# Deferred operand stores, a row scale on another engine and an earlier query load in a two-layer Fourier and attention encoder

## The chip, the cores and the metric

The kernel runs on one core of a Trainium2 chip. The metric is the device time of one execution in microseconds (us), lower is better. A core has five engines that run side by side, each through its own instructions in the order in which they were put on its queue: TensorE (PE in the profile; its weight loads are PEld), VectorE (DVE), ScalarE (ACT), GpSimd (POOL) and SyncE (SP). SP computes nothing here: it issues nearly all the transfers. An engine whose next instruction waits for a semaphore holds up all that stand behind it on its queue.

## The reference

Two sequences go through the same two layers: the prompt with 1024 tokens and the sample with 512, each token 1024 wide. All is float32.

```python
def swiglu_ffn(x, g, w_gate, w_up, w_down):
    h = rms_norm(x, g)
    return (jax.nn.silu(h @ w_gate) * (h @ w_up)) @ w_down
...
for i in range(DEPTH):                      # DEPTH = 2
    if i % 2 == 0:
        x = x + fourier_mixer(x, ...)
    else:
        x = x + attention_mixer(x, ...)
    x = x + swiglu_ffn(x, norm_ffn[i], ffn_w_gate[i], ffn_w_up[i], ffn_w_down[i])
```

The mixer of layer 0 is a grouped Fourier transform followed by a projection. That of layer 1 is attention with 8 query heads on 2 key and value heads of 128 numbers, with normed and rotated queries and keys. The inner width of the SwiGLU block is 2816, in 22 chunks of 128. Since the norm's factor is one number for each token, it can be applied after a product as well as before it: the kernel multiplies gate and up by the row factor r.

## The kernel before

**Numbers in two parts.** A product is made with three matmuls of reduced-precision float32 (`mm3`, L248 to L251): each operand is split into a high part, a copy cast by ACT (L242), and a low part, the difference, on DVE or, where `eng=pool` is given, on POOL (L243). For the weights of the feed-forward block of the sample, `weights_by` (L278) issues the load on SP (L283), casts on ACT (L287) and subtracts on POOL (L288). The raw weights have two buffers, the split ones four.

**Blocks.** Tokens are worked on in blocks of 512: block 0 is the sample, blocks 1 and 2 the prompt. The sample goes through `ffn` (L759), chunk by chunk. The prompt's two blocks go through `ffn_pair` (L924), which makes products of 2 by 2 blocks with seven multiplications (Strassen's scheme in Winograd's form). Its moving operands, seven sums and differences of the normed residual (`OPERANDS`, L35), are made beforehand by `moving` (L871) and stored to DRAM.

**Stages.** `weave` (L1397) interleaves two generators by estimated costs: a main one, marked "F", and an auxiliary one, marked "X". Layer 0's `ffn(0, 0)` runs beside the prompt's mixer and then beside `moving`. When both have ended, `ffn_pair` of layer 0 has TensorE alone. Its tail overlaps the sample's attention (`qkv`, `attend`). Then the sample's output projection and its feed-forward block of layer 1 run beside the prompt's `qkv`, `attend`, output projection and second `moving`. The second `ffn_pair` ends the kernel.

**Order.** The framework that compiles the program puts instructions on each engine's queue in an order of its own, by estimated readiness, with the written order as priority. Where that order has to hold, the code pins an instruction (`pinned`, L256; `keep` in `ffn_pair`). So what is written earlier is not always queued earlier.

**The places that the change touches:**

- `ffn`, L847 to L856, once per chunk, 22 chunks in each of two layers. When the gate product `ga` is complete in PSUM, DVE multiplies it by r (L851) and ACT takes silu into `s` (L853). When the up product is complete, DVE multiplies it by r (L852) and then by `s` (L854). ACT casts the high part and DVE subtracts the low part of `mid` (L856), which the down products read in the next chunks. r lies in SBUF as `first["r"]`, the tile `ss` in the profile.
- `moving`, L877 to L921, four rounds j. A round loads four pieces of the residual (L883), multiplies them by gain and r on DVE (L889) and makes seven operands with `put` (L892): split, then at once a store to DRAM on SP (L905). Low parts of B21, T1, T3 and N4 are made by POOL. B11 and B21 also stay in SBUF (`ring`). The round hands over to the other generator three times (`yield 5.0`): after B11, B21, B22, after T1, T3, and after T2, N4.
- `ffn_pair`, L1175 to L1218. Each step takes the stationary operand made one step before and prepares the next. Hooks run inside steps: `load_rows_down` (L997) loads two rows of down weights in the step T1. `prepare_down` (L1031) starts `operands_down` (L1003) in the step B22: a split on POOL and the sum `s1` on DVE (L1017). The next part of it (L1019, a difference on POOL, and another split) runs in the step T3. The rest is asked for by `product` (L1041).
- `attend`, L1330 to L1394. At the start of each head the query is loaded (L1333, one or two transfers) and split with a low part on POOL (L1335). Then come, for each chunk of 128 queries, the scores (L1343), the softmax on DVE and ACT (L1348 to L1354), the transposes of the probabilities on PE (L1366) and the products with the values.

Of the kernel before, what the change touches and what calls it, by code (L numbers as in the profile page):

```python
# [24 lines left out]
GROUP = NH // NKV  # L25
# [100 lines left out]
def trunk_kernel(ctx: ExitStack, tc: tile.TileContext, t: dict):  # L126
# [632 lines left out]
    def ffn(layer, b, h, out=None):  # L759
# [50 lines left out]
        for fc in range(NF):  # L810
            f0, odd_ = fc - fc % 2, fc % 2
            wg, wu = ready.pop(("gate", fc)), ready.pop(("up", fc))
            if not odd_ and wds is not None:
                want("B", f0 - 2)
                wds.append(ready.pop(("B", f0 - 2)))
            ga, up = bankg(), bankg()
            for dc in range(NC):
                if odd_ and dc == 4:
                    want("A", f0)
                part(wg, h, ga, dc)  # L820
                if here and fc == 0:
                    part(wu, h, up, dc)
                if not odd_ and dc >= 5:
                    one()
                if dc % 2:
                    yield 1.36 if odd_ or dc < 5 else 2.0 if dc == 5 else 2.7
            if odd_:
                want("gate", fc + 1)
                wds = open_items(ms, f0)
            for dc in range(NC):  # L830
                if not odd_ and dc == 3:
                    want("gate", fc + 1)
                if fc == NF - 1 and dc == 4:
                    want("B", f0)
                if dc == (2 if odd_ else 4):
                    want("up", fc + 1)
                if fc == 0 and not here and dc == 1:
                    settled(b)
                if not (here and fc == 0):
                    part(wu, h, up, dc)  # L840
                if not odd_:
                    one(2 if dc in (2, 4, 6) else 1)
                elif dc >= 6:
                    one()
                if dc % 2:
                    yield (3.4 if dc > 1 else 2.7) if not odd_ else 2.7 if dc == 7 else 1.36
            s = tmp()  # L847
            if fc == 0 and not here:
                first["r"] = tl("ss", [TB], F32, "ssF")
                act.copy(first["r"], in_rows(rstd[b]))  # L850
            dve.tensor_tensor(ga, ga, first["r"], op=ALU.mult)  # L851
            dve.tensor_tensor(up, up, first["r"], op=ALU.mult)  # L852
            act.activation(s, ga, AF.Silu)  # L853
            dve.tensor_tensor(up, up, s, op=ALU.mult)  # L854
            m = tl("mid", [2, TB], F32R, "mid")
            split(m[:, 0], m[:, 1], up)  # L856
            if odd_:
                ms.append(m)
            else:
                ms = [m]  # L860
# [10 lines left out]
    def moving(blocks, gain, out, ring, helped):  # L871

        staging = open_pool("mv")
        yield 2.0
        r = [in_rows(rstd[b]) for b in blocks]
        yield 1.0
        for j in range(4):  # L877
            x4 = tl("x", [2, 2, TB], F32, "wX")
            v = {}
            for k in range(2):  # L880
# [11 lines left out]
            def put(name, src):  # L892
# [9 lines left out]
                        room.extend([two[:, 0], two[:, 1]])  # L902
                    x = room.pop(0)
                split(x[:, 0], x[:, 1], src, eng=pool if name in helped else None)
                sp.dma_start(out[name][:, j], x.bitcast(F32))  # L905

            put("B11", v[0, 0])
            put("B21", v[1, 0])
            put("B22", v[1, 1])
            yield 5.0  # L910
            t1 = x4[:, 0, 0]
            dve.tensor_tensor(t1, v[0, 1], v[0, 0], op=ALU.subtract)
            put("T1", t1)
            dve.tensor_tensor(v[0, 1], v[1, 1], v[0, 1], op=ALU.subtract)
            put("T3", v[0, 1])
            yield 5.0
            dve.tensor_tensor(v[1, 1], v[1, 1], t1, op=ALU.subtract)
            put("T2", v[1, 1])
            dve.tensor_tensor(v[1, 0], v[1, 0], v[1, 1], op=ALU.subtract)
            put("N4", v[1, 0])  # L920
            yield 5.0  # L921
        close_pool("mv")

    def ffn_pair(layer, blocks, ring, places, outs):  # L924
# [250 lines left out]
        for f0 in range(0, NF, 2):  # L1175
# [20 lines left out]
                plus(U[i], ps, U[i])  # L1196
            for i, ps in (yield from step("T1", lambda: load_rows_down(f0), 0)):
                plus(V[i], ps, U[i])
            for i, ps in (yield from step("B22", lambda: prepare_down(f0), 0)):
                plus(ps, ps, V[i])  # L1200
                if i == 0:
                    s = gated(1, W, ps)
                else:
                    finish(1, ps, s)
            for i, ps in (yield from step("T3", lambda: next(preps[-1]), 0)):
                plus(U[i], ps, U[i])
                plus(ps, ps, V[i])
                if i == 0:
                    s = gated(2, V[0], ps)
                else:  # L1210
                    finish(2, ps, s)
            for i, ps in (yield from step("N4", None if f0 else lambda: load_acc(blocks[0], 0), 0)):
                plus(ps, ps, U[i])
                if i == 0:
                    s = gated(3, U[0], ps)
                else:
                    finish(3, ps, s)
# [89 lines left out]
    def attend(blocks, straight, slot):  # L1307
# [6 lines left out]
        for g in range(NKV):  # L1314
# [12 lines left out]
                sp.dma_start(vr[:, n * 4 : n * 4 + 4], dv[b][g][:, :, :])  # L1327
            split(vt[:, 0], vt[:, 1], vr, eng=pool)
            yield 1.0
            for h in range(g * GROUP, (g + 1) * GROUP):  # L1330
                qr = raw_tile(T)
                for n, b in enumerate(blocks):
                    sp.dma_start(qr[:, n * TB : (n + 1) * TB], dqk[b][h][:, :])  # L1333
                qt = w_tile(2, T)
                split(qt[:, 0], qt[:, 1], qr, eng=pool)  # L1335
                pts = {}

                def scores(qc):
# [45 lines left out]
                for qc in range(nk + LAG):  # L1384
                    if qc < nk:
                        ps.append(scores(qc))
                        yield 0.7 * nb
                    n = qc - LAG
                    if n >= 0:
# [294 lines left out]
```

## Time and profile before

| | us |
|---|---|
| median of 3 runs | 2942.33 (2935.05 to 2945.19) |
| profiled execution, its own time | 2943.94 |
| its span, first to last instruction | 2942.2 |
| mean granted clock of TensorE | 0.989 |

The profiled execution took 1.74 us more than its span and 1.61 us more than the median. All the rows quoted below belong to it. "PE" rows are matmuls, one row of `mm3` each on L249, L250 and L251. A tile's name before the arrow is what is written, names behind it what is read: `g<-h,w` is a gate or up product of `ffn`, `c<-mid,w` a down product, `a<-ring,w` a product of `ffn_pair`, `a<-w,w` the scores of the prompt's attention.

### The profile page before, as it was taken

How to read it: one execution, taken by the hardware profiler on the slowest of the kernel's cores; microseconds unless marked ns; L12 is line 12 of the kernel's file. 1: busy time of each engine (PE TensorE's matmuls, PEld its weight loads, DVE VectorE, ACT ScalarE, POOL GpSimd, SP SyncE). 2: the span in 40 equal slices, each digit the busy share in tenths (PEclk: the TensorE clock that was granted, in tenths of full speed). 3: DMA queues.
4: the chain of work that ended last, by engine and by line, in shares of the span. 5: the costliest groups of instructions: out<-in, count | busy, mean ns of one | idle time of the engine just before them, and what ended most of it. 6: DMA issues, size and time to landing. Idle time of an engine off the chain costs nothing.

```text
span 2942.2 us, 37189 instructions
## 1 busy us (share of the span) xinstructions
PE 2851.2 (97%) x13656; PEld 2350.9 (80%) x13656; DVE 1737.2 (59%) x3067; ACT 1307.7 (44%) x2134; POOL 1516.2 (52%) x932
## 2 busy tenths in 40 slices
PE   7999999999999999999999999999998999999999
PEld 6778877788888887787777888888886788888887
DVE  6674554466666666836546565563245466666666
ACT  5543233333333333546757777763233333333332
POOL 4334355676776676432332122224535667766774
PEclk8999999999999999999999999999999999999999
DMA  6435475766556653632322112115447865556553
GB/s 219 147 121 161 133 270 188 274 219 218 199 185 207 229 187 111 232 97 86 94 97 90 35 61 78 54 54 179 161 159 279 303 236 202 186 206 226 197 172 116
DMA packets 178870, 490.53 MB, mean 167 GB/s; under 512 B 19488, under 2 KB 29728, under 8 KB 177280
## 3 DMA queue, kind: packets, MB, share of 16 engines
q1 hardware_dynamic: 177760, 483.36, 48.5%
q0 software_dynamic: 640, 3.74, 0.4%
q8 instruction: 108, 1.77, 0.3%
q10 hardware_dynamic: 288, 1.05, 0.1%
q14 instruction: 74, 0.61, 0.1%
HBM read 422.01 MB, written 66.06 MB: 166 GB/s over the span
## 4 chain that ended last, share of the span: by engine, by line
PE 42%; issue 3%; DVE 3%; POOL 2%; ACT 2%; DMA 2%; SPq 0%; POOLq 0%; DVEq 0%; ACTq 0%
PE a L249 6%; PE a L251 6%; PE a L250 6%; PE c L249 5%; PE c L250 4%; PE c L251 4%; PE g L251 3%; PE g L249 3%; PE g L250 3%; PE c L1366 2%; POOL w L288 1%; DVE col L1349 1%; DMA x<-xres 1%; DVE col L1348 1%; DVE acc L1056 1%
## 5 line engine op out<-in xcount | busy, mean ns | idle before, releaser
L288 POOL TENSOR_TENSOR w<-raw,w 128x1024 fp32r<-128x1024 f32 x200 | 479.2, 2403 | 852.0 <-ACT w L287 828.9
L243 POOL TENSOR_TENSOR w<-raw,w 128x512 fp32r<-128x512 f32 (+1 forms) x464 | 607.1, 1328 | 437.8 <-ACT w L242 430.3
L242 ACT CAST w<-raw 128x512 fp32r<-128x512 f32 (+1 forms) x464 | 279.5, 632 | 533.3 <-PE a L251 174.8
L287 ACT CAST w<-raw 128x1024 fp32r<-128x1024 f32 x200 | 208.3, 1048 | 280.6 <-PE g L251 97.0
L249 PE MATMUL g<-h,w 128*128 128x512 f32 x704 | 281.1, 399 | 11.6 <-ACT w L287 6.9
L251 PE MATMUL g<-h,w 128*128 128x512 f32 x704 | 278.3, 395 | 1.2 <-POOL w L288 1.2
L249 PE MATMUL a<-ring,w 128*128 128x512 f32 x708 | 277.5, 392 | 0.0
L250 PE MATMUL g<-h,w 128*128 128x512 f32 x704 | 277.5, 394 | 0.0
L251 PE MATMUL a<-ring,w 128*128 128x512 f32 x708 | 276.0, 390 | 0.0
L250 PE MATMUL a<-ring,w 128*128 128x512 f32 x708 | 275.8, 390 | 0.0
L1056 DVE TENSOR_TENSOR acc<-g,acc 128x512 f32<-128x512 f32 x294 | 201.7, 686 | 105.2 <-PE g L251 104.9
L1056 DVE TENSOR_TENSOR acc<-c,acc 128x512 f32<-128x512 f32 x294 | 201.6, 686 | 93.2 <-PE c L251 91.5
L249 PE MATMUL c<-mid,w 128*128 128x512 f32 x604 | 237.4, 394 | 13.5 <-ACT mid L242 9.5
L250 PE MATMUL c<-mid,w 128*128 128x512 f32 x604 | 236.7, 392 | 1.3 <-DVE mid L243 1.1
L251 PE MATMUL c<-mid,w 128*128 128x512 f32 x604 | 236.4, 392 | 0.0
L249 PE MATMUL c<-h,w 128*128 128x512 f32 x480 | 191.5, 400 | 4.4 <-ACT h L245 3.5
L250 PE MATMUL c<-h,w 128*128 128x512 f32 x480 | 189.7, 396 | 0.4
L251 PE MATMUL c<-h,w 128*128 128x512 f32 x480 | 189.3, 395 | 0.0
L780 DVE TENSOR_TENSOR acc<-c,acc 128x512 f32<-128x512 f32 x176 | 120.8, 688 | 112.6 <-PE c L251 111.9
L249 PEld LDWEIGHTS g<-h,w 128*128 128x128 f32 x704 | 133.7, 190 | 39.3 <-ACT w L287 7.3
L249 PEld LDWEIGHTS a<-ring,w 128*128 128x128 f32 x708 | 133.1, 188 | 32.2 <-DVE mid L243 4.3
L251 PEld LDWEIGHTS g<-h,w 128*128 128x128 f32 x704 | 133.3, 189 | 29.1 <-POOL w L288 2.0
(393 smaller groups left out, 6712.5 us busy)
## 6 DMA issues: line engine op xcount, KB each, us to landing
ring<-mov_B SPq DMA_DIRECT2D x248, 512.0 KB, 5.5
ring<-mov_T SPq DMA_DIRECT2D x88, 512.0 KB, 5.3
raw<-in_gate_dram SPq DMA_DIRECT2D x44, 512.0 KB, 3.5
raw<-in_up_dram SPq DMA_DIRECT2D x44, 512.0 KB, 3.5
raw<-in_down_dram SPq DMA_DIRECT2D x88, 256.0 KB, 3.0
raw<-in_gate_dram SPq DMA_DIRECT2D x88, 256.0 KB, 5.3
raw<-in_up_dram SPq DMA_DIRECT2D x88, 256.0 KB, 5.6
raw<-in_down_dram SPq DMA_DIRECT2D x44, 512.0 KB, 4.2
```

Of the source, the lines that this page charges most:

```text
L242: keep(act.copy(hi, src))
L243: keep(eng.tensor_tensor(lo, src, hi.bitcast(F32), op=ALU.subtract))
L249: pe.matmul(out, lh, rh, start=first, stop=False, **kw)
L250: pe.matmul(out, lh, rl, start=False, stop=False, **kw)
L251: pe.matmul(out, ll, rh, start=False, stop=last, **kw)
L287: pinned(act.copy(flat[:, 0], raw)) if early else act.copy(flat[:, 0], raw)
L288: pool.tensor_tensor(flat[:, 1], raw, flat[:, 0].bitcast(F32), op=ALU.subtract)
L780: dve.tensor_tensor(acc[dc], box[0], acc[dc], op=ALU.add)
L1056: dve.tensor_tensor(acc, chain[d], acc, op=ALU.add)
L1348: dve.tensor_reduce(st[:, 2 * kb : 2 * kb + 1], sc[:, kb], op=ALU.max, axis=AX.X)
L1349: dve.scalar_tensor_tensor(st[:, 1:2], st[:, 2 * nb - 2 : 2 * nb - 1], st[:, 0:1], nrqc[:, gq, h : h + 1], op0=ALU.max, op1=ALU.mult)
L1366: pe.transpose(tr[:, i * P : (i + 1) * P], p[:, kc * P : (kc + 1) * P], ident)
```

## The change

Four edits are made. In `moving` a store is no longer issued by `put`: it goes to a list, and the list is issued at the start of the next third of the round, after the other generator had its turn. In `ffn` the up product is no longer multiplied by r. Instead, GpSimd multiplies silu's result `s` by r in SBUF, and DVE multiplies the up product by that. In `ffn_pair` the first iteration (f0 = 0) runs both parts of `operands_down` one step later, in T3 and N4 in place of B22 and T3. In `attend` the query of the next head of the same group is loaded and split after half the score chunks of the present head (`nk // 2`), where it was done at the start of its own head.

```diff
@@ ffn
             dve.tensor_tensor(ga, ga, first["r"], op=ALU.mult)
-            dve.tensor_tensor(up, up, first["r"], op=ALU.mult)
             act.activation(s, ga, AF.Silu)
+            pool.tensor_tensor(s, s, first["r"], op=ALU.mult)
             dve.tensor_tensor(up, up, s, op=ALU.mult)
@@ moving
+        stores = []
+
+        def flush():
+            for dst, x in stores:
+                sp.dma_start(dst, x.bitcast(F32))
+            stores.clear()
+
         yield 1.0
         for j in range(4):
+            flush()
...
                 split(x[:, 0], x[:, 1], src, eng=pool if name in helped else None)
-                sp.dma_start(out[name][:, j], x.bitcast(F32))
+                stores.append((out[name][:, j], x))
...
             put("B22", v[1, 1])
             yield 5.0
+            flush()
...
             put("T3", v[0, 1])
             yield 5.0
+            flush()
...
             put("N4", v[1, 0])
             yield 5.0
+        flush()
         close_pool("mv")
@@ ffn_pair
-            for i, ps in (yield from step("B22", lambda: prepare_down(f0), 0)):
+            for i, ps in (yield from step("B22", (lambda: prepare_down(f0)) if f0 else None, 0)):
...
-            for i, ps in (yield from step("T3", lambda: next(preps[-1]), 0)):
+            for i, ps in (yield from step("T3", (lambda: next(preps[-1])) if f0 else lambda: prepare_down(0), 0)):
...
-            for i, ps in (yield from step("N4", None if f0 else lambda: load_acc(blocks[0], 0), 0)):
+            for i, ps in (yield from step("N4", None if f0 else lambda: (load_acc(blocks[0], 0), next(preps[-1])), 0)):
@@ attend
-            for h in range(g * GROUP, (g + 1) * GROUP):
+            def query(h):
                 qr = raw_tile(T)
...
                 qt = w_tile(2, T)
                 split(qt[:, 0], qt[:, 1], qr, eng=pool)
+                return qt
+
+            hq = {g * GROUP: query(g * GROUP)}
+            for h in range(g * GROUP, (g + 1) * GROUP):
+                qt = hq.pop(h)
...
                     if qc < nk:
                         ps.append(scores(qc))
+                        if qc == nk // 2 and h + 1 < (g + 1) * GROUP:
+                            hq[h + 1] = query(h + 1)
```

## The prediction, made before the changed kernel had run

> **What bounds the kernel now.** I read the page first, for the shares of the engines.
>
> ```profile
> span 2942.2 us, 37189 instructions
> PE 2851.2 (97%) x13656; PEld 2350.9 (80%) x13656; DVE 1737.2 (59%) x3067; ACT 1307.7 (44%) x2134; POOL 1516.2 (52%) x932
> L251 PE MATMUL g<-h,w 128*128 128x512 f32 x704 | 278.3, 395 | 1.2 <-POOL w L288 1.2
> ```
>
> TensorE is busy for 2851.2 of 2942.2 us, so it is idle for 91.0 us in all. No edit of the diff takes a matmul away: what the change can win is idle time of TensorE and time at a lower granted clock. The third line shows how little the ordinary feed-forward chunks offer: 704 matmuls of gate and up waited 1.2 us in the whole run for a weight split on POOL. Next I read the table by stretches, to see where the 91 us lie.
>
> ```profile
> core 0: us, PE busy (x) PEld busy (x) DVE busy (x) ACT busy (x) POOL busy (x), PEclk, DMA share, GB/s
> 375.00:450.00 75.00, 68.68 (x292) 55.38 (x291) 42.96 (x67) 29.41 (x44) 45.63 (x26) 0.98 0.76 269
> 550.00:1150.00 600.00, 600.00 (x2640) 493.15 (x2639) 387.22 (x600) 217.79 (x392) 426.06 (x301) 1.00 0.62 210
> 1600.00:2000.00 400.00, 387.02 (x2235) 328.53 (x2235) 242.24 (x450) 284.72 (x405) 98.13 (x41) 1.00 0.18 58
> 2240.00:2260.00 20.00, 11.88 (x37) 8.75 (x36) 10.63 (x16) 6.38 (x10) 9.69 (x6) 0.74 0.79 286
> 2285.00:2300.00 15.00, 10.81 (x38) 8.38 (x36) 4.76 (x7) 1.73 (x3) 10.10 (x6) 0.77 0.73 250
> 2300.00:2915.00 615.00, 615.00 (x2702) 505.30 (x2701) 394.74 (x598) 220.96 (x397) 437.32 (x308) 1.00 0.59 205
> ```
>
> In each row the stretch and its length come first, then busy time by engine. The two pair stages (550 to 1150, 2300 to 2915) have TensorE busy all the time at full clock: nothing can be won there. The reach of the change is the first operand stage (375 to 450, 6.3 us idle), the prompt's attention (13.0), and two short places near the second operand stage (8.1 and 4.2). These two also lose clock: 20 us at 0.74 and 15 us at 0.77 are 5.2 and 3.5 us of work not done. The timeline of PE gives the single gaps in brackets, with who ended them; the third of them is at the start of the first pair.
>
> ```profile
> 415.50 0.47 PE L249 MATMUL c<-mid,w 128*128 128x512 f32 x1 [3.17 <-ACT ring L242]
> 444.98 0.50 PE L249 MATMUL c<-mid,w 128*128 128x512 f32 x1 [2.44 <-ACT mid L242]
> 543.30 0.73 PE L249 MATMUL c<-mid,w 128*128 128x512 f32 x2 [2.15 <-ACT mid L242]
> 2248.16 0.80 PE L249 MATMUL g<-h,w 128*128 128x512 f32 x1 [6.89 <-ACT w L287]
> 2292.23 1.22 PE L249 MATMUL c<-mid,w 128*128 128x512 f32 x2 [4.19 <-ACT mid L242]
> ```
>
> So there are five gaps, 18.8 us together. I take the edits to them one by one.
>
> **Stores a third of a round later.** The gap of 6.89 us waits for the cast of gate weights. The queues of SP and POOL ahead of it:
>
> ```profile
> 2230.51 4.40 SPq L905 DMA_DIRECT2D mov_T<-l  x3
> 2237.86 0.32 SPq L905 DMA_DIRECT2D mov_N<-l  x1
> 2238.22 2.23 SPq L883 DMA_DIRECT2D x<-xres  x4
> 2240.49 0.43 SPq L283 DMA_DIRECT2D raw<-in_gate_dram  x1
> ...
> 2230.43 2.41 POOL L288 TENSOR_TENSOR w<-raw,w 128x1024 fp32r<-128x1024 f32 x1
> 2232.80 1.28 POOL L243 TENSOR_TENSOR l<-x,l 128x512 fp32r<-128x512 f32 x1
> 2234.05 2.53 POOL L243 TENSOR_TENSOR w<-raw,w 128x512 fp32r<-128x512 f32 x2
> 2236.53 1.30 POOL L243 TENSOR_TENSOR l<-x,l 128x512 fp32r<-128x512 f32 x1
> ```
>
> SP stood before the store of N4 until POOL had made its low part (2236.53 + 1.30 = 2237.83), then issued the store, the next round's four loads, and only then the gate weights, at 2240.49. The last weight split on POOL before that ended at 2230.43 + 2.41 = 2232.84, so both raw buffers were free 7.65 us before the load went out. A load that much earlier would close the gap of 6.89 and give back the clock. But does the edit do that? It moves the store of N4 by one turn of the other generator, to a place that is still ahead of the next round's loads, and the gate load stood behind these loads too. The order on a queue is also not the written one:
>
> ```profile
> 1535.20 0.86 SPq L1333 DMA_DIRECT2D raw<-dqk  x2
> ...
> 1545.84 3.15 SPq L1333 DMA_DIRECT2D raw<-dqk  x4
> ```
>
> These rows are the first and the last of the prompt's first four queries: two transfers for the first head, four for the third and fourth, all issued within 14 us though written a head apart. A transfer goes out when the compiler takes it to be ready, and the readiness of a store (its low part on POOL) is not changed by a later place in the program. I therefore cost this edit at nothing, and keep both ends: a loss of 1.3 us (one low part later) and a gain of 6.89 + 5.2 = 12.1 us. Nothing reads what is stored before the pair begins, so a late store itself costs nothing as long as feed-forward chunks are left to cover it.
>
> **Row scale on GpSimd.** 44 multiplications leave DVE, 44 come to POOL. The prices, from the list by lines:
>
> ```profile
> L852 DVE TENSOR_TENSOR g<-g,ss 128x512 f32<-128x512 f32 x44 | 30.6, 696 | 30.7 <-PE g L251 30.3
> L243 POOL TENSOR_TENSOR mid<-f,mid 128x512 fp32r<-128x512 f32 x44 | 56.1, 1297 | 5.4 <-ACT mid L242 5.4
> ```
>
> L852 is 0.70 us. POOL's multiplication of this size isn't in the trace, but its subtraction of two SBUF tiles of 128x512 is, at 1.30 us: I take 1.30, so POOL gets 44 x 1.30 = 57 us more and DVE 30.6 less. It stands beside the up product, so it is off the path as long as POOL comes to it before that product's 24 matmuls have ended; a POOL that comes later delays `mid` by what is missing. From the end of the up product to `mid` one DVE instruction less remains. Where TensorE waits for `mid` the saving is real. At the start of the second pair DVE did this:
>
> ```profile
> 2289.45 0.69 DVE L1017 TENSOR_TENSOR s<-raw,raw 128x512 f32<-128x512 f32 x1 [9.51 <-DMA raw<-in_gate_dram]
> 2290.06 0.69 DVE L852 TENSOR_TENSOR g<-g,ss 128x512 f32<-128x512 f32 x1
> 2290.85 0.70 DVE L854 TENSOR_TENSOR g<-g,t 128x512 f32<-128x512 f32 x1
> ```
>
> L854 would start 0.79 us earlier. The gap of 2.15 us at the start of the first pair has the same line behind it, so I take the same there: 1.6 us won. At the gap of 2.44 us L852 also stands ahead of `mid`, but ACT had other casts in front: between nothing and 0.7, I take 0.4. In the attention stage DVE serves the softmax and L852 sits between:
>
> ```profile
> 375.00:450.00 75.00, 2.77 (x4) 0.98 0.76 269
> 1600.00:2000.00 400.00, 6.96 (x10) 1.00 0.18 58
> 2175.00:2260.00 85.00, 2.77 (x4) 0.94 0.73 265
> 1786.40 0.70 DVE g L852
> PE g L251 <- POOL w L243: 2.1, 4, 0.6
> PE a L251 <- POOL w L243: 1.3, 1, 1.3
> ```
>
> The first three lines count L852 alone: 10 of them between 1600 and 2000, and 4 in each operand stage. The fourth is the one that I found on the chain of waits. Between 0.7 and 7.0 us; since one was on the chain, I take 1.0. Against this stands POOL in the operand stages, where by the rows above it had no pause between 2230.43 and 2237.83. One multiplication there makes the low part of N4, its store and all behind it 1.30 late: between nothing and one for each of the 8 chunks of the two operand stages, 10.4 us. I take one, 1.3, since POOL is busy for 45.63 of 75 us there and has room elsewhere.
>
> **First down operands a step later.** In the rows above L1017, the sum of two down rows, held DVE for 9.51 us until its rows had landed, and `mid` was behind it. If it moved behind L854, both gaps (4.19 and 2.15) and 3.5 us of clock would go: 9.8 us. But it was put there, ahead of a product not yet done, because it was taken to be ready; the rows are loaded where they were, so it should be put there again. I take nothing, with 9.8 less the 1.6 above as the other end.
>
> **Queries half a head earlier.** No transfer is added, only its place changes, and the rows above show them issued far ahead already. The waits for a POOL split of this kind are 2.1 and 1.3 us; I take 1.0 of the 3.4, with nothing and 3.4 as ends.
>
> Sum: -1.6 - 0.4 - 1.0 + 1.3 - 1.0 = -2.7 us. The profiled execution's own time was 2943.94 (span 2942.2 and 1.74 around it): 2941.2. Its median lies 1.61 lower, so 2939.6; I say **2939**.
>
> **The clock.** A gap costs more than its length if the granted clock falls:
>
> ```profile
> 405.00:425.00 20.00, 16.83 (x67) 13.37 (x67) 11.43 (x18) 6.90 (x10) 10.77 (x7) 0.91 0.83 302
> 440.00:452.00 12.00, 9.56 (x43) 7.60 (x42) 10.54 (x17) 6.31 (x11) 9.70 (x6) 1.00 0.85 293
> ```
>
> Around the gap of 3.17 us the clock was 0.91 over 20 us (1.8 us lost), around that of 2.44 it was 1.00. So here the step lies between 2.4 and 3.2 us. The gap of 4.19 becomes 3.40 by the sum above and stays past it: its 3.5 us of lost clock are not won. A gap of 2.44 that grows by one multiplication, to 3.74, would cross it. The Trainium skill (TensorE: Matmul & The Clock Gate, section What's actually happening) has the clock fall after a whole idle window of about 3.4 us. By that rule a gap of 3.40 could leave the clock up, and the sum would be 3.5 us lower; but the gap of 3.17 would then have cost no clock, and the trace shows that it did.
>
> **Rivals.**
> *SP is freed* (faster): the gate load goes out before the late store. For it: both raw buffers stood free for 7.65 us. Against it: readiness sets the order. 12.1 us more: 2939 - 12 = 2927.
> *The down sum moves* (faster): 2939 - 8.2 = 2931. For it: later in the program means lower priority. Against it: it was ready by the estimate.
> *POOL becomes the bound in the operand stages* (slower). The multiplication waits on POOL's queue for silu, and the weight splits and low parts stand behind it. For it: POOL's 7.4 us without a pause ahead of the largest gap. Against: 45.63 of 75. It decides once POOL has no pause in most of the 8 chunks; then 8 x 1.30 = 10.4 us, 1.3 of it already in the sum, and two more falls of the clock at 1.8 to 5.2 us each, say 5: 2939 + 9.1 + 5 = 2953.
> *The clock stays up* after the shortened gap of 3.40 us: 2939 - 3.5 = 2936. Against it: the gap of 3.17.
> *The change does not do what it says*: queues come out as before and POOL's price eats DVE's gain: 2943.
>
> **How the numbers follow.** A measurement of this kernel can tell about 0.3%, 8.8 us, from no change: below 2933.5 is faster, above 2951.1 slower. Chances: forecast 0.40, clock up 0.04, SP freed 0.20, down sum 0.13, POOL 0.17, nothing done 0.06. Faster is SP freed, most of the down sum (0.11) and a tail of the forecast (0.03): 0.34. Slower is most of POOL: 0.14 and a tail of 0.02: 0.16. The rest, 0.50, is the same. The range goes from 2925, below SP freed, to 2954, just above POOL. It leaves out both faster rivals together (2919), and POOL with more than two falls of the clock, under 2 in 10 together.
>
> **What would show it.** Right: 44 rows of POOL at L854's place of about 1.3 us and none of L852; the gap near 2248 still there and ended by the gate cast; L1017 still just ahead of the last up multiplication, with gaps near 3.4 and 1.4 us. Wrong: the gate load ahead of the store of N4 and a clock of 1.00 there (SP freed); L1017 behind `mid`; or weight splits late behind POOL's multiplication, with PE waiting for L288 by more than 1.2 us. The compiler's order may also shift elsewhere, in the 1150 to 1600 stretch above all, for which I have no term.

## The result and the profile after

| | before | changed |
|---|---|---|
| median, us (14 runs each) | 2939.89 (2933.71 to 2945.32) | 2934.45 (2932.45 to 2939.76) |
| ratio, 95% interval | | 0.9983 (0.9975 to 0.9991) |
| profiled execution, us | 2943.94 | 2934.45 |
| its span, mean granted clock | 2942.2, 0.989 | 2932.7, 0.992 |

The change is worth 5 us, 0.17%: inside the 0.3% that counts as no change, yet with an interval below 1. The two profiled executions lie 9.5 us apart because that of before is 4.05 us above the median of its 14 runs and that of the changed kernel is its median. So about 4 us of the difference between the two traces are chance, and the traces have to be compared by stretches.

The page of the changed kernel, whole span: shares of the engines, then groups by line.

```profile
PE 2843.5 (97%) x13656; PEld 2347.7 (80%) x13656; DVE 1717.8 (59%) x3023; ACT 1304.9 (44%) x2134; POOL 1574.1 (54%) x976
...
L249 PE MATMUL c<-mid,w 128*128 128x512 f32 x604 | 238.2, 395 | 16.1 <-ACT mid L242 8.1
L250 PE MATMUL c<-mid,w 128*128 128x512 f32 x604 | 237.3, 393 | 2.9 <-DVE mid L243 2.9
```

TensorE has the same 13656 matmuls. DVE has 44 instructions fewer, POOL 44 more. TensorE stood idle for 16.1 us ahead of the first rows of down products (L249), 8.1 of it waiting for the high part of `mid`, and for 2.9 us ahead of L250, waiting for its low part alone. On the page of before these were 13.5, 9.5 and 1.1 us. The list by lines gives the moved multiplication's price:

```profile
L853 POOL TENSOR_TENSOR t<-t,ss 128x512 f32<-128x512 f32 x44 | 56.8, 1292 | 26.5 <-ACT t L852 26.4
```

Next the table by stretches, first before, then changed. The columns are those of the prediction: the stretch, its length, PE, PEld, DVE, ACT, POOL, granted clock, DMA share and rate. The three stretches are the first operand stage with the start of the first pair, the prompt's attention, and the second operand stage with the start of the second pair.

```profile
375.00:560.00 185.00, 176.53 (x766) 144.11 (x765) 83.15 (x126) 60.94 (x88) 106.40 (x56) 0.99 0.64 221
...
1600.00:2000.00 400.00, 387.02 (x2235) 328.53 (x2235) 242.24 (x450) 284.72 (x405) 98.13 (x41) 1.00 0.18 58
...
2175.00:2320.00 145.00, 131.74 (x555) 105.84 (x555) 72.15 (x119) 50.34 (x80) 84.58 (x50) 0.94 0.76 268
```

```profile
375.00:560.00 185.00, 177.97 (x774) 145.44 (x773) 77.68 (x118) 61.32 (x90) 118.92 (x67) 0.99 0.66 224
...
1600.00:2000.00 400.00, 385.72 (x2217) 326.73 (x2216) 234.17 (x428) 279.12 (x396) 114.60 (x53) 1.00 0.19 61
...
2175.00:2320.00 145.00, 134.50 (x575) 108.45 (x574) 66.95 (x101) 51.09 (x83) 97.45 (x60) 0.96 0.82 288
```

Idle time of TensorE is the length less PE's busy time; clock lost is the length times what is missing to 1.00 (the clock is given in hundredths, so this is good to about 1 us). In the second operand stage idle time falls from 13.3 to 10.5 us and lost clock from 8.7 to 5.8: 5.7 us won. In the first, idle time falls from 8.5 to 7.0: 1.4 won. In attention it rises from 13.0 to 14.3: 1.3 lost.

Something is lost outside the table too. From 95 to 375 us, where the sample's first feed-forward block runs beside the prompt's mixer, idle time rises from 5.0 to 7.4 us. The list of waits of that stretch has a row in the changed kernel that before has not (us in all, times, longest):

```profile
PE c L249 <- DVE acc L780: 2.4, 3, 1.3
```

Three times a down product waits for DVE's running sum of down products. At the longest of these waits, DVE's queue has a mixer instruction (L482) ahead of the sum, where before it had it behind. All eight kernels of this document with GpSimd's multiplication have this row at 2.4 to 2.6 us, the five with the multiplication of before have none. It is a price of the row scale.

The timeline of PE in the changed kernel shows the single gaps, in brackets:

```profile
414.13 0.77 PE L249 MATMUL c<-mid,w 128*128 128x512 f32 x1 [3.75 <-ACT ring L242]
...
441.62 0.50 PE L249 MATMUL c<-mid,w 128*128 128x512 f32 x1 [0.69 <-ACT mid L242]
...
540.31 0.50 PE L249 MATMUL c<-mid,w 128*128 128x512 f32 x1 [1.92 <-ACT mid L242]
...
2241.90 1.22 PE L249 MATMUL c<-mid,w 128*128 128x512 f32 x2 [5.45 <-ACT mid L242]
...
2284.34 0.80 PE L250 MATMUL c<-mid,w 128*128 128x512 f32 x1 [2.69 <-DVE mid L243]
```

Against before: 3.17 became 3.75, 2.44 became 0.69, 2.15 became 1.92, 6.89 became 5.45 and is now a wait for `mid` in place of gate weights, and 4.19 became 2.69, a wait for the low part only.

The fourth stretch lies between the end of the first pair and attention. The same two matmuls stand at its ends in both kernels, first before, then changed:

```profile
1210.93 0.50 PE L249 MATMUL a<-mid,w 128*128 128x512 f32 x1 [1.73 <-DVE acc L1056]
...
1516.78 1.22 PE L317 MATMUL c<-dg,ones 128*128 128x128 f32 x4 [2.20 <-ACT t L1277]
```

```profile
1208.34 0.50 PE L249 MATMUL a<-mid,w 128*128 128x512 f32 x1 [1.73 <-DVE acc L1067]
...
1511.32 0.71 PE L317 MATMUL c<-dg,ones 128*128 128x128 f32 x4 [2.35 <-ACT t L1288]
```

That is 305.85 us before and 302.98 after, 2.9 won at the same granted clock. In the first 95 us, where both kernels run the same work, the changed execution has about 2.5 us less of idle time and lost clock: that is chance, and not the edits.

### The profile page after: what moved, and what is told of

It is laid out like the page before. It is cut to its first block, busy times and chain, and to the rows that moved or that the text cites. A ratio compares the mean times of both kernels' runs of the same rounds, so it can differ in the third digit from the quotient of the medians.

```text
span 2932.7 us, 37209 instructions
## 1 busy us (share of the span) xinstructions
PE 2843.5 (97%) x13656; PEld 2347.7 (80%) x13656; DVE 1717.8 (59%) x3023; ACT 1304.9 (44%) x2134; POOL 1574.1 (54%) x976
## 4 chain that ended last, share of the span: by engine, by line
PE 42%; DVE 4%; issue 2%; DMA 2%; POOL 2%; ACT 2%; SPq 0%; ACTq 0%; POOLq 0%; DVEq 0%
PE a L249 6%; PE a L251 6%; PE a L250 6%; PE c L249 5%; PE c L250 5%; PE c L251 5%; PE g L251 3%; PE g L250 3%; PE g L249 3%; PE c L1382 2%; DVE col L1365 1%; DVE col L1364 1%; POOL w L288 1%; DVE acc L1067 1%; POOL l L243 0%
## 5 line engine op out<-in xcount | busy, mean ns | idle before, releaser
L249 PE MATMUL g<-h,w 128*128 128x512 f32 x704 | 279.0, 396 | 3.9 <-DVE ss L339 2.0
L249 PE MATMUL a<-ring,w 128*128 128x512 f32 x708 | 277.4, 392 | 0.0
L251 PE MATMUL g<-h,w 128*128 128x512 f32 x704 | 276.1, 392 | 0.0
L250 PE MATMUL g<-h,w 128*128 128x512 f32 x704 | 276.1, 392 | 0.0
L251 PE MATMUL a<-ring,w 128*128 128x512 f32 x708 | 276.0, 390 | 0.0
L250 PE MATMUL a<-ring,w 128*128 128x512 f32 x708 | 275.8, 390 | 0.0
L249 PE MATMUL c<-mid,w 128*128 128x512 f32 x604 | 238.2, 395 | 16.1 <-ACT mid L242 8.1
L250 PE MATMUL c<-mid,w 128*128 128x512 f32 x604 | 237.3, 393 | 2.9 <-DVE mid L243 2.9
L251 PE MATMUL c<-mid,w 128*128 128x512 f32 x604 | 237.0, 393 | 1.2 <-POOL w L288 1.2
L249 PE MATMUL c<-h,w 128*128 128x512 f32 x480 | 191.1, 400 | 2.0 <-ACT h L245 1.5
L250 PE MATMUL c<-h,w 128*128 128x512 f32 x480 | 189.1, 395 | 0.5 <-DVE h L246 0.3
L251 PE MATMUL c<-h,w 128*128 128x512 f32 x480 | 188.7, 394 | 0.0
L249 PEld LDWEIGHTS a<-ring,w 128*128 128x128 f32 x708 | 133.0, 188 | 32.0 <-DVE mid L243 4.4
L249 PEld LDWEIGHTS g<-h,w 128*128 128x128 f32 x704 | 132.6, 188 | 30.7 <-DVE ss L339 2.2
L251 PEld LDWEIGHTS a<-ring,w 128*128 128x128 f32 x708 | 133.0, 188 | 27.9
```

The costliest lines, as they stand in the source:

```text
L249: pe.matmul(out, lh, rh, start=first, stop=False, **kw)
L250: pe.matmul(out, lh, rl, start=False, stop=False, **kw)
L251: pe.matmul(out, ll, rh, start=False, stop=last, **kw)
```

## Experiments: each edit alone

My theory after the result (A): the row scale carries the gain of the operand stages. Rivals: it is worth no more than the terms of the prediction (B), or the other three edits give the gain (C). Four kernels take one edit each.

**Row scale alone.**

```diff
-            dve.tensor_tensor(up, up, first["r"], op=ALU.mult)
             act.activation(s, ga, AF.Silu)
+            pool.tensor_tensor(s, s, first["r"], op=ALU.mult)
```

> The kernel before with the row scale alone moved to GpSimd, on silu's result; stores, first down operands and queries as before. Theory A (the row scale carries the gain): 44 rows of POOL near 1.3 us at that line and none of the DVE multiplication of up; the gap of 2.44 us at 444.98 in the first operand stage gone, the gap of 4.19 at 2292.23 near 3.4 or less; time 4 to 6 us below before (ratio 0.998 to 0.9985). Theory B (the row scale is worth only my three terms, 1.6 + 0.4 + 1.0 less 1.3 for POOL): 1.7 us below, ratio 0.9994, and the gaps of the operand stages change by under 0.8 us each. Theory C (the other edits give the gain, POOL costs): no gain or up to 10 us above, with PE waiting for weight splits on POOL.

Measured: 2937.77 us against 2938.26, ratio 0.9992 (0.9983 to 1.0001). Two gaps on the timeline of PE and a row of the table by stretches:

```profile
445.86 0.50 PE L249 MATMUL c<-mid,w 128*128 128x512 f32 x1 [0.49 <-DVE acc L780]
...
2290.14 0.50 PE L250 MATMUL c<-mid,w 128*128 128x512 f32 x1 [1.79 <-DVE mid L243]
```

```profile
2175.00:2320.00 145.00, 135.64 (x586) 109.53 (x585) 70.24 (x117) 51.73 (x83) 96.05 (x58) 0.96 0.79 278
```

This one edit makes the changes at these places that the whole change makes: the gap of 2.44 us is gone, that of 4.19 is 1.79, idle time in the second operand stage is 9.4 us, and attention has 14.4 idle. The three waits of 2.4 us beside the mixer are there too. As a mechanism A holds. Its size, 4 to 6 us, does not: the interval reaches only 5 us, and its middle is 2.3, near B.

**Deferred stores alone** (the hunks in `moving`).

```diff
-                sp.dma_start(out[name][:, j], x.bitcast(F32))
+                stores.append((out[name][:, j], x))
```

> The kernel before with the deferred operand stores alone. Theory A (stores cost and give nothing): ratio 0.9996 to 1.0004, the gap of 6.89 us at 2248.16 still there within 1.3 us and still ended by the cast of gate weights. Theory C (the late stores free SP for the weight loads): that gap at 1.5 us or less, the clock around it 1.00, time 5 to 12 us below (ratio 0.996 to 0.998).

Measured: 2941.37, ratio 1.0010 (1.0000 to 1.0020). The gap for gate weights stays:

```profile
2248.50 0.79 PE L249 MATMUL g<-h,w 128*128 128x512 f32 x1 [5.97 <-ACT w L287]
```

Nothing is freed: C falls for the stores. The ratio's middle lies above the 0.9996 to 1.0004 of theory A. On SP's queue the order of stores and loads is that of before in the second operand stage, and only a few change places in the first.

**First down operands a step later, alone.**

```diff
-step("B22", lambda: prepare_down(f0), 0)
+step("B22", (lambda: prepare_down(f0)) if f0 else None, 0)
...
-step("T3", lambda: next(preps[-1]), 0)
+step("T3", (lambda: next(preps[-1])) if f0 else lambda: prepare_down(0), 0)
```

> The kernel before with the first down operands a step later, alone. Theory A (the sum of two down rows is put at the same place by its readiness): the DVE row L1017 still just ahead of the last up multiplication, gaps of 2.15 and 4.19 us as before, ratio 0.9997 to 1.0003. Theory C (it moves behind the last mid): the gaps at 543.30 and 2292.23 gone, time 8 us below (ratio 0.997).

Measured: 2939.27, ratio 1.0006 (0.9996 to 1.0017). The gap near 2292 is 4.48 us, and on DVE's queue the sum of two down rows (L1017) still stands just ahead of the last up multiplication: it did not move, and C falls here too.

Both of these runs lose something in the first operand stage. The gap that was 2.44 us before is 4.45 with the deferred stores alone and 3.84 with the later down operands alone. From 375 to 560 us both have 9.7 us idle at a clock of 0.97, where before had 8.5 at 0.99. How an edit of the later pair stage comes to lengthen that gap was not traced.

**Earlier queries alone.**

```diff
                         ps.append(scores(qc))
+                        if qc == nk // 2 and h + 1 < (g + 1) * GROUP:
+                            hq[h + 1] = query(h + 1)
```

> The kernel before with the earlier query loads alone. Theory A (queries were already issued far ahead): SP order nearly the same, up to 1 us below (ratio 0.9996 to 1.0000), TensorE's idle time between 1150 and 2000 us within 1 us of the 13.0 us plus what lies before 1600. Theory C (the queries give the 3 us that the whole change won between 1209 and 1514 us): time 3 us below (ratio 0.999), with fewer gaps between 1200 and 1550.

Measured: 2937.33, ratio 0.9997 (0.9988 to 1.0006). But its trace has the gain between the two landmarks:

```profile
1203.82 0.50 PE L249 MATMUL a<-mid,w 128*128 128x512 f32 x1 [1.75 <-DVE acc L1056]
...
1506.75 0.71 PE L317 MATMUL c<-dg,ones 128*128 128x128 f32 x4 [2.29 <-ACT t L1277]
```

302.93 us, where the row scale alone has 305.85 and the later down operands alone 305.11. The traces of all the runs of this document agree: eight kernels with the earlier queries take 302.9 to 303.9 us between the landmarks, the five without 305.1 to 306.2. The only exception is the last combination below, which has the queries and takes 306.02, with a granted clock of 0.67 in the first 10.2 us, 3.4 us of work. So the 2.9 us there belong to the queries, as C had it for this stretch, though ratio and idle time came out as theory A had them. Listed idle time hardly shows it: 2.6 of the 2.9 us lie in PE's busy time, 292.17 us before (1534 matmuls) and 289.59 here (1535). Why nearly the same matmuls are busy for less time stays open. Waits for the POOL split (L251 `g<-w,w`), on which I had based the term, fall only from 2.1 to 1.2 us.

## Experiments: which edits the change needs

Single edits give 0.9992 x 1.0010 x 1.0006 x 0.9997 = 1.0005, the whole 0.9983. Either the edits work together, or four intervals of 0.0009 each way add up. Three combinations tell.

**Without the store deferral** and **without the row scale**: the changed kernel with that one edit undone as in the diffs above.

> The changed kernel without the deferred stores: row scale on GpSimd, first down operands a step later, earlier queries. Theory A (stores give nothing): ratio 0.998 to 0.999, as the changed kernel. Theory E (the deferral costs alone, 1.001, but helps beside the row scale): slower than 0.999.

> The changed kernel without the row scale: deferred stores, first down operands a step later, earlier queries. Theory A (the row scale carries the gain of the operand stages): the gap near 442 back at 2.4 us or more and the one near 2288 back at 4 us or more with 6.8 us of half clock; ratio 0.9995 to 1.002. Theory C (the others give it): ratio 0.998 to 0.999.

Measured: without the deferral 2935.37, ratio 0.9985 (0.9977 to 0.9994); without the row scale 2938.05, ratio 0.9995 (0.9986 to 1.0003). The deferral gives nothing beside the others. Without the row scale the gaps near 442 and 2288 are back, at 4.12 and 4.52 us. The first is longer than the 2.44 us of before, as it was with the deferred stores or the later down operands alone. With the row scale it is 0.69 us beside both: so here the row scale also takes away what these two edits cost.

**Row scale and queries, nothing else.**

> The kernel before with two edits alone, the row scale on GpSimd and the earlier queries. Theory F (these two carry the whole gain, about 0.0010 each; the deferred stores and the later down operands are worth nothing beside them): ratio 0.998 to 0.999, the same as the changed kernel's 0.9983. Rival (the two edits without weight, stores and down operands, are needed beside the row scale): 0.9992 or above, as the row scale alone.

Measured: 2933.51 against 2939.93, ratio 0.9976 (0.9965 to 0.9986). Theory F holds: two edits carry the whole gain; the ratio's middle is a little beyond its 0.998. If the four edits add, equal weights for the eight ratios (four single edits, three combinations, the whole) give by least squares: row scale -3.4 us, queries -2.7, stores +1.2, down operands +0.9, each about 2 us either way. The eight residuals are 0.0006 at most, inside the intervals, so the times need no interaction to explain them, though the gap near 442 shows one. Whether the last two edits cost 1 to 2 us or nothing stays open.

## Experiments: why GpSimd, and what holds the second operand stage

**Row scale on silu's result, but by DVE.** Is the shorter way to `mid` the gain, or an engine with less work? The edit is made on the kernel with the row scale alone.

```diff
-            pool.tensor_tensor(s, s, first["r"], op=ALU.mult)
+            dve.tensor_tensor(s, s, first["r"], op=ALU.mult)
```

> The kernel before with the row scale on silu's result, as in the changed kernel, but by VectorE instead of GpSimd: DVE does 44 multiplications at 0.70 us as before, POOL gets none, and the multiplication still leaves the end between the up product and mid. Theory A (the shorter end at mid is what the row scale wins; GpSimd only carries it): the gap at 444.98 gone, the gap of 4.19 at 2292.23 near 1.8, as in the run with the row scale alone; attention no longer 1.4 us longer; time 2 to 5 us below before (ratio 0.998 to 0.9993). Theory B (a DVE with less work wins it): ratio 1.000 and the gaps as in before. If POOL's extra work costs, this run is faster than the run with the row scale alone.

Measured: 2944.01 against 2939.09, ratio 1.0019 (1.0009 to 1.0029), slower than before. The expectation's price was wrong. From the list by lines, and the timeline at the start of the second pair:

```profile
L853 DVE TENSOR_TENSOR t<-t,ss 128x512 f32<-128x512 f32 x44 | 64.5, 1467 | 31.6 <-ACT t L852 31.5
```

```profile
2280.99 2.40 POOL L288 TENSOR_TENSOR w<-raw,w 128x1024 fp32r<-128x1024 f32 x1 [3.10 <-ACT w L287]
2281.43 2.50 DVE L853 TENSOR_TENSOR t<-t,ss 128x512 f32<-128x512 f32 x1 [2.01 <-ACT t L852]
...
2288.62 2.33 POOL L1150 TENSOR_TENSOR raw<-raw,raw 128x1024 f32<-128x1024 f32 x1
2289.51 1.99 DVE L1017 TENSOR_TENSOR s<-raw,raw 128x512 f32<-128x512 f32 x1 [3.97 <-DMA raw<-in_down_dram]
```

The multiplication takes 1.47 us on average, not 0.70, though engine, size and type are as in L852 of before. What differs is where `up` and `s` lie: L852 read PSUM and SBUF, this one reads SBUF twice. In both places shown, DVE's instruction begins beside a POOL one and ends 0.54 to 0.55 us after it (2281.43 + 2.50 = 2283.93 against 2283.39; 2291.50 against 2290.95): it stands still until POOL is done. The prompt's attention has the control, the same instruction with no POOL instruction beside it:

```profile
1638.23 0.68 DVE L853 TENSOR_TENSOR t<-t,ss 128x512 f32<-128x512 f32 x1
```

Of the 44, the 16 that meet no POOL instruction take 0.67 to 0.69 us each; the longest that meets one takes 2.66. The Trainium skill (SBUF — State Buffer, section Who interferes with whom) says that a DVE instruction with two SBUF inputs and a GpSimd instruction that reads SBUF exclude each other, and that the one that began first keeps the port to its end. The trace agrees, with 1.47 us on average for the 0.68 alone. The gaps say the rest: the longest wait of the second operand stage is now for `mid`, 6.17 us, as in the kernels with POOL's multiplication, but the one near 2292 is 4.38. So neither theory came out as written, and this run can't tell the shorter way from the relief of DVE: it shortens the one and loads the other. What it shows is that the place on silu's result was a gain on POOL, at 1.29 us, and not on DVE, at 1.47.

**Loads of x ahead of the late stores.** The largest gap, 5.45 us, is still there. The chain that ended last in the changed kernel, around it (start, length, what):

```profile
2232.27 1.26 POOL l L243
2233.54 0.32 SPq L880
...
2235.20 4.60 DMA x<-xres
...
2239.82 0.06 DVE x L897
...
2240.48 0.70 DVE g L854
...
2241.26 0.59 ACT mid L242
```

POOL ends the low part of N4, SP stores it, and only behind that store loads the next round's x. DVE's multiplication of x by gain (L897) waits for that load, and L854, which only wants TensorE's product and POOL's result, stands behind it on DVE. Theory D: the store of N4 on SP is the cause.

```diff
         for j in range(4):
-            flush()
             x4 = tl("x", [2, 2, TB], F32, "wX")
...
                     v[d, k] = x
+            flush()
```

> The changed kernel with one place moved: the stores of T2 and N4 are issued behind the next round's four loads of x instead of ahead of them. Theory D (the store of N4, which waits for POOL's low part, holds the loads of x on SP; the DVE gain of x that waits for them, L897, holds mid): the gap of 5.45 us near 2236 falls to 2 us or less and the clock around it stays near 1.00; with the gate weights still behind the stores, 3 to 8 us below the changed kernel's 0.9983, so a ratio to before of 0.9955 to 0.9973. Rival (the gate weights or POOL are late anyway): the gap stays above 4 us, ended by a cast of weights, ratio 0.998 to 0.999.

Measured: 2936.70, ratio 0.9995 (0.9985 to 1.0005), no better than the changed kernel's 0.9983. Timeline of PE and of SP's queue:

```profile
2213.69 1.57 SPq L880 DMA_DIRECT2D mov_T<-l  x2
2215.30 0.44 SPq L283 DMA_DIRECT2D raw<-in_gate_dram  x1
2215.80 2.25 SPq L890 DMA_DIRECT2D x<-xres  x4
...
2221.27 0.79 PE L249 MATMUL g<-h,w 128*128 128x512 f32 x1 [3.30 <-ACT w L287]
...
2240.57 0.50 PE L249 MATMUL c<-mid,w 128*128 128x512 f32 x1 [2.79 <-ACT w L287]
```

The gap at 2236 goes, but gate weights now stand behind the stores of T1 and T3, which wait for POOL too, and TensorE waits 3.30 and 2.79 us for casts of weights. Idle time between 2175 and 2320 rises to 15.0 us. D had the cause of the gap right and the cure wrong: on one queue, whichever load is behind the waiting store is late.

**Stores of T2 and N4 a third of a round later.**

```diff
         for j in range(4):
-            flush()
             x4 = tl("x", [2, 2, TB], F32, "wX")
```

> The changed kernel with the flush at the top of a round left out, so that the stores of T2 and N4 go out with those of the next round's first third, behind the loads of x and, by their place, behind the next gate weights too. Theory D (SP's order is what makes the gap near 2236: the store of N4 holds loads that are due): the gap goes without the 3.30 and 2.79 us gaps for weights that the run with the loads first had, idle time between 2175 and 2320 us at 6 us or less, half clock there at 3.4 us or less, ratio 0.996 to 0.998. Rival (weights still stand behind stores, or POOL is late by itself): idle time there at 10 to 15 us, ratio 0.998 to 1.000.

Measured: 2934.49 against 2939.93, ratio 0.9983 (0.9974 to 0.9992).

```profile
375.00:560.00 185.00, 181.31 (x802) 149.13 (x800) 81.99 (x132) 63.32 (x95) 121.38 (x69) 1.00 0.69 238
...
2175.00:2320.00 145.00, 128.85 (x539) 103.71 (x538) 62.36 (x94) 47.03 (x72) 92.69 (x57) 0.95 0.80 286
```

The two operand stages answer in opposite ways: the first falls to 3.7 us idle at full clock, the second rises to 16.2. For the second stage the rival holds, and its 10 to 15 us were even too low; the longest of the waits there is for a cast of weights:

```profile
2241.84 0.50 PE L249 MATMUL c<-mid,w 128*128 128x512 f32 x1 [4.68 <-ACT w L287]
```

**Stores issued by ScalarE's queue.**

```diff
-                sp.dma_start(dst, x.bitcast(F32))
+                act.dma_start(dst, x.bitcast(F32))
```

> The changed kernel with the operand stores issued by ScalarE's queue instead of SP's; 56 issues leave SP. Theory D (a store on SP that waits for POOL's low part holds the loads behind it): no load of x or weights waits any more, idle time between 2175 and 2320 us at 6 us or less, ratio 0.996 to 0.998. Price: each issue takes 0.3 to 0.5 us of the issuing queue, and ScalarE's casts stand behind a store that waits; if that decides, PE waits for casts on ACT (L242, L287) and the ratio is 0.999 to 1.003.

Measured: 2945.70, ratio 1.0021 (1.0009 to 1.0032). Timeline near the largest gap:

```profile
2253.05 2.50 POOL L243 TENSOR_TENSOR l<-x,l 128x512 fp32r<-128x512 f32 x2 [4.34 <-ACT l L242]
...
2254.35 1.55 ACTq L880 DMA_DIRECT2D mov_T<-l  x2
...
2256.47 0.58 ACT L242 CAST mid<-g 128x512 fp32r<-128x512 f32 x1
...
2257.83 0.79 PE L249 MATMUL g<-h,w 128*128 128x512 f32 x1 [5.95 <-DVE mid L243]
```

The price named in the expectation decides: the cast of `mid` stands behind stores that wait for POOL, and TensorE waits 5.95 us. On both queues the waiting store held what was behind it. (This profiled execution took 2955.1 us, 9 more than the median of its runs.)

**The parts that paid, together.** Row scale and queries; in layer 0 the stores as in the run with the stores of T2 and N4 a third later, in layer 1 at once as before. Against the kernel before, the lines for the stores are:

```diff
                 split(x[:, 0], x[:, 1], src, eng=pool if name in helped else None)
-                sp.dma_start(out[name][:, j], x.bitcast(F32))
+                stores.append((out[name][:, j], x))
+                if not late:
+                    flush()
...
-        yield from moving((1, 2), g_ffn[layer], mov[layer], ring, ("B21", "T1", "T3", "N4"))
+        yield from moving((1, 2), g_ffn[layer], mov[layer], ring, ("B21", "T1", "T3", "N4"), layer == 0)
```

> Row scale on GpSimd and earlier queries, no later down operands, and the stores of T2 and N4 a third later in the first operand stage alone; the second operand stage has its stores where the kernel before had them. Theory (the parts add where they do not meet): the first operand stage as in the run with the stores a third later (idle time between 375 and 560 us 3.7 us, no lower clock there), the second as in the run with row scale and queries alone (8.8 us idle, 5.1 us of work lost to the clock), so 5 us below that run's 0.9976: a ratio to before near 0.996. Rival (a gap won in one stage comes back, as it did in the runs with the loads first): 0.9975 or above, with idle time between 375 and 560 us at 6 us or more, or more than 12 us between 2175 and 2320.

Measured: 2929.28 (6 runs) against 2938.15, ratio 0.9968 (0.9956 to 0.9980): faster than both kernels by its middle, and 0.3% below before.

```profile
375.00:560.00 185.00, 180.85 (x792) 148.53 (x792) 80.46 (x123) 62.30 (x92) 119.76 (x68) 0.99 0.68 235
...
2175.00:2320.00 145.00, 134.33 (x570) 108.46 (x569) 67.19 (x102) 49.74 (x77) 97.87 (x61) 0.96 0.85 300
```

The first stage has 4.2 us idle, the second 10.7. The two stages can be set one by one. The second came out 1.9 us above the run with row scale and queries alone (8.8), which is 0.0006 of the time: so 0.9968 and not 0.996. The intervals of that run and of the changed kernel overlap this one's, so it isn't shown to be faster than either.

## Why the prediction came out as it did

It said 2939 and "same"; measured were 2934.45 and a ratio of 0.9983. The forecast lay 4.6 us high. 2.4 of them are its base: the three runs shown had a median of 2942.33, 14 runs have 2939.89. Another 2.7 are the sum, -2.7 us against -5.4 by the medians; rounding 2939.6 down to 2939 took 0.6 off. That the total came so near is in part luck: gains that were put too low stand against losses that had the wrong sign or no term. Its terms:

- *Row scale, second pair's start (-0.8)*: mis-sized, and its step was wrong. I had L854 start one DVE instruction earlier with the sum of two down rows (L1017) still ahead of it, and a gap of 3.40. The timeline shows another order. Once `up` needs no multiplication first, L854 stands ahead of that sum (presumably because the compiler takes it to be ready earlier); the sum now stands between L854 and the low part:

```profile
2278.77 0.70 DVE L854 TENSOR_TENSOR g<-g,t 128x512 f32<-128x512 f32 x1 [5.48 <-PE g L251]
...
2282.53 1.16 DVE L1028 TENSOR_TENSOR s<-raw,raw 128x512 f32<-128x512 f32 x1 [3.06 <-DMA raw<-in_down_dram]
2283.61 0.68 DVE L243 TENSOR_TENSOR mid<-g,mid 128x512 fp32r<-128x512 f32 x1
```

  The gap is 2.69 us. This is the rival "the down sum moves" in part, through an edit that I had not connected with it: the run with the row scale alone shows it at 1.79 us, the run with the later down operands alone does not. The run with DVE's multiplication on silu's result has the same order, so the order comes from the place and not from the engine. How long the gap is then goes by when the down rows land: 0.57 us with row scale and queries, 4.38 with DVE's multiplication.
- *Row scale, first pair's start (-0.8)*: mis-sized; 2.15 became 1.92, and 1.80 with the row scale alone.
- *Row scale at 444.98 (-0.4)*: mis-sized; 1.75 us went (2.44 to 0.69).
- *Row scale in attention (-1.0)*: wrong sign. Six kernels with DVE's multiplication of before or of the variant have 12.6 to 13.2 us idle between 1600 and 2000, the eight with POOL's have 14.0 to 14.5. DVE has less to do there, but `mid` was not what the 13 us waited for. That POOL's longer step causes the extra 1.3 us fits this split. In the lists of waits most of it is on two rows: transposes that wait for ACT's `t`, 1.3 us before and 2.1 after, and scores that wait for ACT's `p`, 5.3 and 5.6. How POOL's step delays these was not traced.
- *POOL in the operand stages (+1.3)*: no net cost there; the 2.4 us that the row scale cost lie beside the mixer, for which I had no term. The gap near 412 did grow from 3.17 to 3.75 (4.08 with the row scale alone), but the two stages together won 7 us in the profiles. The rival in which POOL becomes the bound did not come.
- *Stores (0)*: right within the noise, and for the order on SP right in reason: a later place in the program leaves it nearly as it was. The longer gap near 442 was not foreseen, 4.45 us in the run with the stores alone. What a real move does to that order, the runs with other places show.
- *Down operands (0)*: right within the noise, alone 1.0006 with 1 inside the interval; the gap of 3.84 us near 442 was not foreseen here either.
- *Queries (-1.0)*: mis-sized, 2.9 us in the traces and 2.7 by the eight ratios, and most of it not at the waits that I named. I had argued from the queue rows of the prompt's queries, but the prompt's attention has 12.9 us idle with the edit and 13.0 without: the gain lies in the stretch of the sample's attention.

The largest miss is outside these terms: for the 6.89 us gap I had no term from the row scale. In the five kernels with the multiplication on POOL and this stage's stores at once or as in the change, idle time from 2175 to 2320 is 8.8 to 10.7 us; in the five with DVE's multiplication of before, 12.3 to 14.1. What I said would show the forecast right came out in part: 44 rows of 1.29 us, no L852, a gap near the old place. But `mid` ends it, and L1017 has moved.

## What to carry to other kernels

An instruction taken out of the way between two engines can be worth more or less than its time where a list scheduler sets the queues: here the new order won in the second operand stage and lost 2.4 us beside the mixer. See which instruction it lets pass, and what then stands behind a transfer. A store that waits for a slow engine holds every load behind it on its queue; moving it pays only where the load that it lets through is the one that is due, so try each stage by itself. Before an operation goes from PSUM operands to two SBUF operands on VectorE, look at what GpSimd does beside it.

## What the runs showed of the hardware

I had put the step of the clock between gaps of 2.4 and 3.2 us. That was wrong: the same gap can leave the clock up or not. One gap of attention, before and with the queries alone, with the 10 us around it in the table by stretches:

```profile
1635.55 0.50 PE L249 MATMUL a<-w,w 128*128 128x512 f32 x1 [2.11 <-ACT p L1352]
```

```profile
1632.00:1642.00 10.00, 7.64 (x43) 6.13 (x42) 6.58 (x13) 8.56 (x11) 0.00 (x0) 1.00 0.14 51
```

```profile
1624.45 0.79 PE L249 MATMUL a<-w,w 128*128 128x512 f32 x1 [2.12 <-ACT p L1357]
```

```profile
1621.00:1631.00 10.00, 7.88 (x39) 6.52 (x37) 6.59 (x13) 7.42 (x10) 0.00 (x0) 0.83 0.13 47
```

A gap of 2.11 us at 1.00, one of 2.12 at 0.83, which is 1.7 us of work. The Trainium skill (TensorE: Matmul & The Clock Gate, section What's actually happening) has activity windows of about 3.4 us that run freely, so that the moment of a change of the clock depends on where in a window the first matmul falls. The two rows fit that for a fall as well, but no run here shows the windows' edges. It also has the clock at half after at least one idle window of about 3.4 us. If that means a window without any work, the trace contradicts it: 2.12 us cannot fill 3.4.

The start shows the same. In the first 95 us, where these kernels run the same work, the granted clock was 0.84 before and 0.93 with the queries alone, 8.6 us of work apart. The runs of before show what that does to the time: of the 27 beside the run with row scale and queries, the fastest, 2934.00 us, had a mean granted clock of 0.993 and the slowest, 2945.51, one of 0.989. The difference, 0.004 of 2940 us, is 11.8 us, about all of that spread. So the profiles alone, one execution each, are not enough to size an edit.
